# Experts with several row blocks, run one block at a time with small experts between, in a two-layer mixture-of-experts backbone

## The chip, the cores and the metric

The kernel runs on one core of one Trainium2 chip. The metric is the device time of one execution in microseconds (us); the kernel before is shown by the median of three runs. The profile is of one further execution. Engines are called by their names: TensorE (PE in the rows, PEld its weight loads), VectorE (DVE), ScalarE (ACT), GpSimd (POOL) and SyncE (SP), whose queue issues the weight loads.

## The reference

Two layers over 512 latent tokens and 256 context tokens of width 1024, all in float32. Each layer has a token mixer (projection, convolution, recurrence, output projection) and then a mixture of experts, which is what the change touches:

```python
gate = p_group * top_p / jnp.sum(top_p, axis=-1, keepdims=True)        # top-1 group of 4, top-2 of its 8 experts
...
def expert_block(args):
    x_blk, e = args
    a, u = jnp.split(x_blk @ w_gu[e], 2, axis=-1)                      # w_gu[e]: 1024 x 1024
    return (jax.nn.silu(a) * u) @ w_down[e]                            # w_down[e]: 512 x 1024
...
out = jnp.zeros((n_tok + 1, d), t.dtype).at[row_tok].add((yb * row_gate[:, None]).astype(t.dtype))
```

Layer 0 sends 768 tokens through two experts each, layer 1 only the 512 latent ones. Every one of the 32 experts' weights, 6 MB each, is read in each layer.

## The kernel before

The kernel runs mixer, routing and experts of layer 0, then the same of layer 1, then a last norm. In the routing, the experts are sorted on the chip by their number of rows, and each rank has a fixed room (`rooms`): in layer 0 rank 0 has 320 rows, rank 1 192, rank 2 128, ranks 3 to 5 96, ranks 6 to 15 64, ranks 16 to 28 32; in layer 1 rank 0 has 160, ranks 1 to 3 96, ranks 4 to 11 64, ranks 12 to 28 32. Three experts ("static") are not ranked; they are loaded while the routing still runs and computed first. Rows beyond a room go through `overflow`, a branch behind the last-but-one expert, whose count is tested at run time.

`units` cuts a rank's room into blocks of 128, then 64 and 32 rows: rank 0 of layer 0 is 128 + 128 + 64, rank 1 is 128 + 64, ranks 3 to 5 are 64 + 32. For a block, `rows_in` gathers its rows from the normed tokens in HBM (an indirect DMA of GpSimd, L1189) and transposes them on TensorE (L1211; VectorE copies the result to `xT`, L1213). `gate_up` multiplies them with four weight chunks (L1226 for 128 rows, L1230 for 64 or 32), `activate` makes silu(a) * u and transposes it (the h-transposes, L1244 for 128 rows, L1253 else; for 128 rows ScalarE and VectorE work first, L1239 to L1241), and `down` multiplies with the last two chunks (L1283 and L1295 in layer 0, L1321 and L1333 in layer 1). In layer 0 the result is scaled and scattered to HBM (L1181); in layer 1 the rows of several blocks of a kind are collected in one of three accumulators (`YB`) and added to the tokens by a matmul with a one-hot matrix (`merge`, L1369 to L1383).

An expert's weights are six chunks of 1 MB: four of gate and up, two of down. `load_chunks` issues them on SP in the program's order (L1162), each into a slot; `ring` takes slots from the head of a list and puts them back at its end, so a slot is used again when the others have been used, and its load waits on SP until the last matmul that reads it is done. The list has 16 slots in layer 0 (one more holds the modulation) and 17 in layer 1.

`moe` walks the ranks in `order`, a list by hand for each layer. For each expert, all its units are gathered and transposed, and each chunk is multiplied with all the units before the next chunk (`start`). In `end`, the units' activations come first, then their downs; before the last unit's down, `between` starts the next expert (its load on SP, its transposes and its first chunk), if `ahead` finds that the PSUM banks do (layer 0: fewer than three banks beside the first 128-block's own; layer 1: one unit of 64 or 32). The other three chunks of the next expert follow. SP alone is scheduled by hand (`manual_schedule`); the order of the other engines comes from the framework and follows the program closely. `flush` in layer 1 merges what is left of a kind when no unit of it is to come.

```python
    order = [[6, 16, 7, 17, 0, 18, 19, 1, 20, 21, 2, 22, 8, 3, 23, 9, 4, 24, 10, 5, 25, 11, 12, 26, 13, 14, 27, 15, 28],
             [4, 12, 5, 13, 0, 14, 15, 1, 16, 6, 17, 2, 18, 7, 19, 3, 20, 8, 21, 9, 22, 10, 23, 11, 24, 25, 26, 27, 28]]
```

Of the kernel before, what the change touches and what calls it, by code (L numbers as in the profile page):

```python
# [33 lines left out]
class Backbone:  # L34
# [1129 lines left out]
                self.tc.keep_in_program_order(o)  # L1164
        return list(tiles)

    def ring(self, n=6):

        out = []
        for _ in range(n):  # L1170
            pool, name = self.slots.pop(0)
            self.slots.append((pool, name))
            out.append(pool.tile([128, 2, D], F32, name=name))
        return out

# [124 lines left out]
    def down_here(self, kind, hT, dn, idx, pool, ps, last):  # L1300


        nc = self.nc
        tok, gate = idx
        f = 128 // kind
        w = D // f
        grp = self.groups.setdefault(kind, [])
        e = len(grp)
        if not grp:
            self.YB.append(self.YB.pop(0))  # L1310
            self.into[kind] = self.YB[-1]
        YB = self.into[kind]
        grp.append(tok)
        if len(grp) == f:
            self.tokens(kind, pool)
        if f == 1:
            for h in range(2):
                c = slice(512 * h, 512 * h + 512)
                py = ps.tile([128, 512], F32, name="acc", bufs=3)
                for k in range(4):  # L1320
                    nc.tensor.matmul(py, hT[k], dn[k // 2][:, k % 2, c], start=k == 0, stop=k == 3)  # L1321
                nc.vector.scalar_tensor_tensor(YB[:, c], py, gate, self.m5[:, c], op0=OP.mult, op1=OP.mult)
        else:
            py = ps.tile([128, 512], F32, name="acc", bufs=3)
            part = [(slice(kind * ((e - u) % f), kind * ((e - u) % f) + kind), slice(w * u, w * u + w)) for u in range(f)]
            for k in range(4):
                if k == 2 and last:

                    for _ in range(10):
                        nc.tensor.matmul(ps.tile([128, 512], F32, name="pS", bufs=2), self.onesb,  # L1330
                                         self.onesb[:, 0:1].to_broadcast([128, 512]), start=True, stop=True)
                for pr, c in part:
                    nc.tensor.matmul(py[pr, :w], hT[k], dn[k // 2][:, k % 2, c], start=k == 0, stop=k == 3)  # L1333
            for pr, c in part:
                nc.vector.scalar_tensor_tensor(YB[pr, c], py[pr, :w], gate[pr], self.m5[pr, c], op0=OP.mult, op1=OP.mult)
        if len(grp) == f:
            self.merge(kind, ps)
# [112 lines left out]
    def moe(self, l, stat, xp, mp, ps, ms2):  # L1450
        tc, nc, io = self.tc, self.nc, self.io
        if l:
# [5 lines left out]
            self.OT = mp.tile([128, 4, 512], F32R, name="OT")  # L1458
            self.YR = mp.tile([128, 2, D], F32R, name="YR")
            self.groups, self.into = {}, {}  # L1460
        left = [u[0] for r in self.order[l] for u in self.units(l, r)]

        def flush():

            for kind in list(self.groups):
                if kind not in left:
                    self.tokens(kind, mp)
                    self.merge(kind, ps)

        order = self.order[l]  # L1470
        ws = {}

        def load(n):
            if n not in ws:
                r = order[n]
                e = nc.sync.value_load(self.eid[0:1, r:r + 1], min_val=32 * l, max_val=32 * l + 31)
                ws[n] = self.load_expert(e, self.ring())

        def begin(n):
            load(n)  # L1480
            return self.start(ws[n], self.units(l, order[n]), xp, ps)

        N = len(order)
        for b in stat[:-1]:
# [2 lines left out]
        for n in range(-1, N):  # L1487

            nxt = []
            fits = n + 1 < N - 1 and self.ahead(l, self.units(l, order[n + 1]))  # L1490
            self.end(cur, mp, ps, n == N - 1, (lambda: nxt.append(begin(n + 1))) if fits else None)
            if l and n >= 0:
                for u in self.units(l, order[n]):
                    left.remove(u[0])
                flush()
            if n + 1 == N - 1:
                load(n + 1)
                self.overflow(l, xp, mp, ps, ms2)
            if n + 1 < N:
                cur, rest = nxt[0] if nxt else begin(n + 1)  # L1500
                rest()
# [105 lines left out]
    def dbgout(self, l, **k):  # L1607
        for n, t in k.items():
            if f"{n}{l}" in self.dbg:
# [7 lines left out]
             [160, 96, 96, 96] + [64] * 8 + [32] * 17 + [0] * 3]  # L1617

    static = [[7, 8, 9], [7, 8, 9]]
    order = [[6, 16, 7, 17, 0, 18, 19, 1, 20, 21, 2, 22, 8, 3, 23, 9, 4, 24, 10, 5, 25, 11, 12, 26, 13, 14, 27, 15, 28],  # L1620
             [4, 12, 5, 13, 0, 14, 15, 1, 16, 6, 17, 2, 18, 7, 19, 3, 20, 8, 21, 9, 22, 10, 23, 11, 24, 25, 26, 27, 28]]
    NOV = 28

    def plan(self):
# [141 lines left out]
```

## Time and profile before

| | |
|---|---|
| three runs | 2007.62, 2000.01, 2010.29 us; median 2007.62 |
| the profiled execution | 1996.57 us; span 1994.8 us |
| TensorE busy / its mean granted clock | 1700.2 us (85%) / 0.945 |
| VectorE, ScalarE, GpSimd busy | 914.0 (46%), 458.2 (23%), 394.3 us (20%) |
| moved by DMA | 542.35 MB, mean 272 GB/s |
| weight chunks into ring slots, issued by SP | 242 of gate/up, 121 of down, 1024 KB each |

The times of a row count from the start of the span. A row of the timeline gives start, duration, engine, line, operation, output and inputs, shape and number of instructions, and in brackets how long the engine was idle before it and what ended that. A float32 matmul of the program stands as two in the trace. Busy time of TensorE holds the pipelined ends of matmuls, which are modelled, so its share is no measure of its throughput. DMA share is the mean busy share of the core's 16 DMA engines.

### The profile page before, as it was taken

The numbers are of one execution on the slowest core, as the hardware profiler recorded it, in microseconds if no ns is written. First come the engines' busy times: TensorE is split into PE (matmuls) and PEld (weight loads), VectorE is DVE, ScalarE is ACT, GpSimd is POOL, SyncE is SP. The second block draws the span as 40 slices with busy tenths as digits, with TensorE's granted clock in tenths as the row PEclk, the third lists the DMA queues.
The fourth block names the chain that finished last, engine by engine and source line by source line (L and its number), as shares of the span: only waits on it lengthen the run. The fifth ranks groups of instructions, "written<-read, shape, count | busy, mean of one in ns | idle before, by whom it ended". The sixth has DMA issues, their size and how long they took to land. (4 is left out here: it accounts for less than half of the span.)

```text
span 1994.8 us, 33498 instructions
## 1 busy us (share of the span) xinstructions
PE 1700.2 (85%) x13488; PEld 1098.2 (55%) x13488; DVE 914.0 (46%) x2141; ACT 458.2 (23%) x897; POOL 394.3 (20%) x308
## 2 busy tenths in 40 slices
PE   5998999999968999888875899898968898888885
PEld 2766778798843444333332688777754344334342
DVE  4425255635664132222322637666563644445444
ACT  3512223323212122122211533333320100110011
POOL 1502212111122111111110632222111211111110
PEclk8999999999988999999987899999987999999998
DMA  7376562263489979999997322114478989999995
GB/s 276 101 271 212 179 212 76 76 242 90 168 326 374 418 317 379 417 416 418 417 419 298 135 82 57 54 43 157 137 280 324 417 342 417 418 417 418 417 418 241
DMA packets 141513, 542.35 MB, mean 272 GB/s; under 512 B 17394, under 2 KB 66720, under 8 KB 85417
## 3 DMA queue, kind: packets, MB, share of 16 engines
q1 hardware_dynamic: 118408, 466.17, 59.1%
q10 hardware_dynamic: 15040, 55.08, 8.0%
q0 software_dynamic: 7904, 18.90, 2.5%
q8 instruction: 108, 1.77, 0.4%
q14 instruction: 53, 0.43, 0.1%
HBM read 530.95 MB, written 15.96 MB: 274 GB/s over the span
## 5 line engine op out<-in xcount | busy, mean ns | idle before, releaser
L1230 PE MATMUL acc<-w,xT 128*32 128x256 f32 (+1 forms) x3360 | 378.4, 454 | 59.1 <-DVE xT L1213 34.6
L1230 PEld LDWEIGHTS acc<-w,xT 128*32 128x32 f32 (+1 forms) x3360 | 135.2, 119 | 260.6 <-issue 159.0
L322 POOL TENSOR_TENSOR hilo<-raw,hilo 128x1024 fp32r<-128x1024 f32 x64 | 157.3, 2463 | 436.4 <-ACT hilo L319 396.7
L333 PE MATMUL acc<-HA,hilo 128*128 128x384 f32 (+1 forms) x960 | 204.7, 355 | 0.0
L333 PE MATMUL acc<-HB,hilo 128*128 128x384 f32 (+1 forms) x960 | 202.4, 353 | 0.0
L333 PEld LDWEIGHTS acc<-HA,hilo 128*128 128x128 f32 x960 | 168.8, 189 | 16.2 <-issue 4.2
L333 PEld LDWEIGHTS acc<-HB,hilo 128*128 128x128 f32 x960 | 171.0, 190 | 9.2 <-issue 0.8
L1250 ACT COPY au<-acc 128x256 f32<-128x256 f32 (+1 forms) x69 | 31.1, 453 | 594.3 <-PE acc L1230 551.9
L345 PE MATMUL acc<-hilo,HA 128*128 128x512 f32 x504 | 131.2, 412 | 12.8 <-POOL HA L283 6.3
L1189 POOL DMA_INDIRECT xb<-h,idx x63 | 65.7, 1043 | 385.7 <-PE pS L1211 357.1
L345 PE MATMUL acc<-hilo,HB 128*128 128x512 f32 x504 | 125.8, 398 | 3.9 <-DVE hilo L322 3.6
L345 PEld LDWEIGHTS acc<-hilo,HA 128*128 128x128 f32 x504 | 97.9, 198 | 41.0 <-POOL HA L283 7.5
L1274 DVE SCALAR_TENSOR_TENSOR au<-w,gt,au 32x256 f32<-32x256 f32 (+2 forms) x102 | 58.6, 577 | 114.1 <-ACT au L1273 111.7
L319 ACT CAST hilo<-raw 128x1024 fp32r<-128x1024 f32 x80 | 83.5, 1049 | 119.1 <-PE acc L345 27.5
L345 PEld LDWEIGHTS acc<-hilo,HB 128*128 128x128 f32 x504 | 94.5, 190 | 29.1 <-DVE hilo L322 4.5
L1295 PE MATMUL acc<-w,hT 128*32 128x256 f32 (+1 forms) x816 | 97.2, 478 | 12.4 <-DVE hT L1258 6.4
L389 DVE TENSOR_TENSOR Q<-Q,Dk 128x256 f32<-128x256 f32 (+1 forms) x144 | 89.6, 651 | 23.7 <-PE pA L464 11.8
L1333 PE MATMUL acc<-w,hT 128*32 128x256 f32 (+1 forms) x896 | 87.4, 440 | 7.3 <-DVE hT L1258 5.2
L1181 POOL DMA_INDIRECT yb<-ys,idx x39 | 39.7, 1019 | 260.9 <-DVE ys L1297 185.3
L384 DVE TENSOR_TENSOR K<-K,Dk 128x768 f32<-128x768 f32 x64 | 72.9, 1139 | 21.5 <-ACT tmp L401 17.9
L1295 PEld LDWEIGHTS acc<-w,hT 128*32 128x32 f32 (+1 forms) x816 | 37.4, 126 | 69.5 <-issue 51.3
L1297 DVE TENSOR_TENSOR ys<-acc,au 128x256 f32<-128x256 f32 (+1 forms) x34 | 18.4, 542 | 124.9 <-PE acc L1295 124.5
(369 smaller groups left out, 2245.5 us busy)
## 6 DMA issues: line engine op xcount, KB each, us to landing
w<-in_w_e_gu SPq DMA_DIRECT2D x242, 1024.0 KB
w<-in_w_e_down SPq DMA_DIRECT2D x121, 1024.0 KB
adaw<-in_w_ada ACTq DMA_DIRECT2D x40, 1024.0 KB
raw<-in_w_in SPq DMA_DIRECT2D x64, 512.0 KB
adaw<-in_w_ada SPq DMA_DIRECT2D x8, 1024.0 KB
raw<-in_w_out SPq DMA_DIRECT2D x16, 512.0 KB
HA<-in_w_e_gu SPq DMA_DIRECT2D x6, 1024.0 KB
h<-SG SPq DMA_DIRECT2D x10, 512.0 KB
```

Of the source, the lines that this page charges most:

```text
L319: nc.scalar.copy(W[:, 0], w)
L322: eng.tensor_sub(W[:, 1], w, W[:, 0].bitcast(F32))
L333: nc.tensor.matmul(o, W[:, wi, k, :], H[k // 4][:, k % 4, hi, t], start=k == 0 and wi == hi, stop=k == 7 and wi == 1)
L345: nc.tensor.matmul(pa, H[k // 4][:, k % 4, hi, t], W[k // 2][:, wi, k % 2, :], start=k == ks[0] and wi == hi, stop=k == ks[-1] and hi == 1)
L384: nc.vector.tensor_tensor(half(Kv, TOK, 0, kn, b), half(Kv, TOK, 0, kn, b), vw(Dv, b, [[2 * b, n], [TOK - b, 2], [0, b]]), op=OP.mult)
L389: nc.vector.tensor_tensor(o, o, vw(Dv, (TOK + b) * d, [[2 * b, qn // (2 * b)], [0, b]]), op=OP.mult)
L1181: st = nc.gpsimd.indirect_dma_start(out=rows, out_offset=bass.IndirectOffsetOnAxis(ap=idx, axis=0), in_=yb, in_offset=None, bounds_check=r ...
L1189: self.nc.gpsimd.indirect_dma_start(out=xb, out_offset=None, in_=rows, in_offset=bass.IndirectOffsetOnAxis(ap=idx, axis=0), bounds_check=r ...
L1230: nc.tensor.matmul(pg[kind * u:kind * u + kind, :w], xT[k], gu[:, k % 2, w * u:w * u + w], start=st, stop=sp)
L1274: nc.vector.scalar_tensor_tensor(ms[pr, :o], self.m5s[pr, 0, c], g0[pr], ms[pr, :o], op0=OP.mult, op1=OP.add)
L1295: nc.tensor.matmul(py[kind * u:kind * u + kind, :w], hT[k], dn[k // 2][:, k % 2, w * u:w * u + w], start=k == 0, stop=k == 3)
L1333: nc.tensor.matmul(py[pr, :w], hT[k], dn[k // 2][:, k % 2, c], start=k == 0, stop=k == 3)
```

## The change

An expert that stands more than once in `order` is run one unit at a time: each time but the last it stands there takes its next unit, the last takes the rest. Its weights are loaded at its first step; their six slots are taken out of the ring's list (`keep`) and put back at its end after its last step. Experts between these steps use the slots that remain. In layer 0 the order is new: rank 1 stands twice (its 128 rows, then rank 23, then its 64), rank 0 three times (128; ranks 26, 17; 128; rank 16; 64), and all others have other places than before. In layer 1, rank 0 stands twice, with rank 14 between its 128 and its 32 rows; the rest is as before. The accumulator of a merge is now the first that no other kind is using.

```diff
-    def ring(self, n=6):
+    def ring(self, n=6, keep=None):
...
             pool, name = self.slots.pop(0)
-            self.slots.append((pool, name))
+            (self.slots if keep is None else keep).append((pool, name))
             out.append(pool.tile([128, 2, D], F32, name=name))
...
-            self.YB.append(self.YB.pop(0))
+            busy = [id(self.into[k]) for k in self.groups if k != kind]
+            self.YB.append(self.YB.pop([id(t) in busy for t in self.YB].index(False)))
...
-        left = [u[0] for r in self.order[l] for u in self.units(l, r)]
+
+        order, steps = self.order[l], []
+        for n, r in enumerate(order):
+            k, us = order[:n].count(r), self.units(l, r)
+            end = r not in order[n + 1:]
+            steps.append((r, us[k:] if end else us[k:k + 1], end))
+        left = [u[0] for st in steps for u in st[1]]
...
-        ws = {}
+        ws, kept = {}, {}
 
         def load(n):
-            if n not in ws:
-                r = order[n]
+            r = order[n]
+            if r not in ws:
                 e = nc.sync.value_load(self.eid[0:1, r:r + 1], min_val=32 * l, max_val=32 * l + 31)
-                ws[n] = self.load_expert(e, self.ring())
+                if not steps[n][2]:
+                    kept[r] = []
+                ws[r] = self.load_expert(e, self.ring(keep=kept.get(r)))
 
         def begin(n):
             load(n)
-            return self.start(ws[n], self.units(l, order[n]), xp, ps)
+            return self.start(ws[order[n]], steps[n][1], xp, ps)
...
-            fits = n + 1 < N - 1 and self.ahead(l, self.units(l, order[n + 1]))
+            fits = n + 1 < N - 1 and self.ahead(l, steps[n + 1][1])
             self.end(cur, mp, ps, n == N - 1, (lambda: nxt.append(begin(n + 1))) if fits else None)
-            if l and n >= 0:
-                for u in self.units(l, order[n]):
+            if n >= 0:
+                r, us, end = steps[n]
+                if end:
+                    self.slots += kept.pop(r, [])
+                for u in us:
                     left.remove(u[0])
-                flush()
+                if l:
+                    flush()
...
-    order = [[6, 16, 7, 17, 0, 18, 19, 1, 20, 21, 2, 22, 8, 3, 23, 9, 4, 24, 10, 5, 25, 11, 12, 26, 13, 14, 27, 15, 28],
-             [4, 12, 5, 13, 0, 14, 15, 1, 16, 6, 17, 2, 18, 7, 19, 3, 20, 8, 21, 9, 22, 10, 23, 11, 24, 25, 26, 27, 28]]
+
+
+    order = [[15, 24, 1, 23, 1, 6, 19, 3, 4, 18, 25, 12, 0, 26, 17, 0, 16, 0, 28, 2, 13, 7, 21, 10, 5, 14, 11, 9, 20, 8, 22, 27],
+             [4, 12, 5, 13, 0, 14, 0, 15, 1, 16, 6, 17, 2, 18, 7, 19, 3, 20, 8, 21, 9, 22, 10, 23, 11, 24, 25, 26, 27, 28]]
```

## Rows read from the trace of the kernel before

**Rows 1.** Windows: span, busy time (instructions) by engine; clock, DMA share, GB/s.

```profile
700.00:740.00 40.00, 35.84 (x248) 17.25 (x247) 16.56 (x30) 12.47 (x24) 8.10 (x8) 1.00 0.74 292
760.00:780.00 20.00, 18.50 (x78) 7.65 (x80) 6.88 (x12) 4.83 (x8) 3.04 (x3) 1.00 0.82 328
1620.00:1640.00 20.00, 18.00 (x134) 9.52 (x132) 11.35 (x38) 1.80 (x4) 3.56 (x3) 1.00 0.59 226
```

**Rows 2.** TensorE's waits, the longest group, in 616:1003 and then in 1003:1088.

```profile
PE acc L1230 <- DVE xT L1213: 17.4, 18, 1.5
...
PE acc L1230 <- DMA w<-in_w_e_gu: 14.3, 5, 5.5
```

**Rows 3.** TensorE's timeline in layer 0, h-transposes of single steps.

```profile
626.05 0.75 PE L1253 MATMUL pS<-ident,au 128*128 128x128 f32 x4 [0.69 <-ACT au L1250]
636.62 0.51 PE L1253 MATMUL pS<-ident,au 128*128 128x128 f32 x2 [0.55 <-ACT au L1250]
...
661.16 0.51 PE L1253 MATMUL pS<-ident,au 128*128 128x128 f32 x2 [0.55 <-ACT au L1250]
...
730.10 0.50 PE L1253 MATMUL pS<-ident,au 128*128 128x128 f32 x2 [0.49 <-ACT au L1250]
...
737.73 0.51 PE L1253 MATMUL pS<-ident,au 128*128 128x128 f32 x2 [0.54 <-ACT au L1250]
...
783.06 0.50 PE L1253 MATMUL pS<-ident,au 128*128 128x128 f32 x2 [0.49 <-ACT au L1250]
...
790.69 0.51 PE L1253 MATMUL pS<-ident,au 128*128 128x128 f32 x2 [0.54 <-ACT au L1250]
...
814.27 1.13 PE L1244 MATMUL pS<-ident,au 128*128 128x128 f32 x4 [2.88 <-DVE au L1241]
...
829.81 0.51 PE L1253 MATMUL pS<-ident,au 128*128 128x128 f32 x2 [0.49 <-ACT au L1250]
...
842.01 0.74 PE L1253 MATMUL pS<-ident,au 128*128 128x128 f32 x4 [0.74 <-ACT au L1250]
...
861.19 1.07 PE L1253 MATMUL pS<-ident,au 128*128 128x128 f32 x6
...
874.09 0.51 PE L1253 MATMUL pS<-ident,au 128*128 128x128 f32 x2 [0.49 <-ACT au L1250]
...
975.22 0.75 PE L1253 MATMUL pS<-ident,au 128*128 128x128 f32 x4 [0.74 <-ACT au L1250]
...
990.31 0.75 PE L1253 MATMUL pS<-ident,au 128*128 128x128 f32 x4 [0.74 <-ACT au L1250]
```

**Rows 4.** TensorE's timeline at the end of layer 0's experts.

```profile
1053.23 3.42 PE L1230 MATMUL acc<-w,xT 128*64 128x512 f32 x8 [5.55 <-DMA w<-in_w_e_gu]
...
1082.48 0.50 PE L1253 MATMUL pS<-ident,au 128*128 128x128 f32 x2 [0.53 <-ACT au L1250]
1085.21 1.93 PE L1295 MATMUL acc<-w,hT 128*32 128x256 f32 x32 [2.23 <-DVE hT L1258]
```

**Rows 5.** SP's timeline: issues of four chunks, from the first's start to the last's end.

```profile
696.39 30.87 SPq L1162 DMA_DIRECT2D w<-in_w_e_gu  x4
...
984.49 8.40 SPq L1162 DMA_DIRECT2D w<-in_w_e_gu  x4
...
1000.40 9.14 SPq L1162 DMA_DIRECT2D w<-in_w_e_gu  x4
...
1607.71 27.96 SPq L1162 DMA_DIRECT2D w<-in_w_e_gu  x4
```

**Rows 6.** DMA issues: count, size of each, median us from issue to landing.

```profile
w<-in_w_e_down POOLq DMA_DIRECT2D x2, 1024.0 KB, 6.1
```

**Rows 7.** TensorE's timeline in layer 1, rank 0 and the first wait for weights.

```profile
1598.42 3.60 PE L1226 MATMUL pA<-w,xT 128*128 128x512 f32 x8
...
1634.20 1.93 PE L1333 MATMUL acc<-w,hT 128*32 128x256 f32 x32
...
1943.15 1.43 PE L1230 MATMUL acc<-w,xT 128*32 128x256 f32 x16 [2.96 <-DMA w<-in_w_e_gu]
```

More of the change, by code (lines that the diff above doesn't have):

```diff
@@ L1468, in flush @@
                     self.merge(kind, ps)
-        order = self.order[l]
-        ws = {}
+        ws, kept = {}, {}
         def load(n):
-            if n not in ws:
-                r = order[n]
+            r = order[n]
+            if r not in ws:
                 e = nc.sync.value_load(self.eid[0:1, r:r + 1], min_val=32 * l, max_val=32 * l + 31)
-                ws[n] = self.load_expert(e, self.ring())
+                if not steps[n][2]:
+                    kept[r] = []
+                ws[r] = self.load_expert(e, self.ring(keep=kept.get(r)))
         def begin(n):
             load(n)
-            return self.start(ws[n], self.units(l, order[n]), xp, ps)
+            return self.start(ws[order[n]], steps[n][1], xp, ps)
         N = len(order)
```

## The prediction

> **What bounds the kernel now.** The shares of the whole span say little, so I read by stretch. Each mixture-of-experts stretch (layer 0 from about 616 to 1087 us, layer 1 from 1536 to 1974) is fed by one stream of 1 MB weight chunks, six to an expert. First look at the windows [rows 1]: between the ends of these stretches the DMA share is 1.0 but for three places, 0.74 over 40 us, 0.82 and 0.59 over 20 us each. These holes are worth 10.4 + 3.6 = 14.0 us in layer 0 and 8.2 us in layer 1, and each follows an expert with many rows (ranks 0 and 1 of layer 0, rank 0 of layer 1). Then ask who is late. In the sums of TensorE's waits [rows 2] the first 387 us of layer 0 have seven groups and none is a weight's landing; the largest is the copy of the transposed rows. Only after 1003 us does TensorE wait for weights, 14.3 us in five waits. So until 1003 TensorE is behind the stream, the ring is full, and a hole is the stream waiting for a slot; behind 1003 small experts let TensorE catch up and the stream ends the layer. Both limits lie close together: a change that closes holes but makes TensorE slower gains nothing.
>
> **Price of a step on TensorE.** The step of one unit is best priced from one unit's h-transposes to the next step's [rows 3], because everything, waits too, lies in between: 32 rows after 32 take 7.6 us (730.10 to 737.73), 64 after 32 12.2, 32 after 64 10.6, 64 after 64 15.1, 96 after 64 19.2, 32 after 96 12.9. Rank 2, the only 128-block that runs alone, takes 23.6 from the 32 before it and 15.5 to the 32 after it. Rank 1 (128 and 64 together) takes 45.3 from 32 to 32 and rank 0 (128, 128, 64 together) 68.9. Subtract 7.6 for the pair of 32s: a lone 128-block costs 31.5 us, a 64 between 32s 15.2; but rank 0 in company costs 61.3, which leaves (61.3 - 15.2) / 2 = 23.0 for each of its blocks. The 8.5 us between them is the wait that another unit's matmuls cover when they stand beside it (2.88 us for VectorE in front of rank 2's transposes [rows 3]), and a hand-over to the next step.
>
> **The change in layer 0: TensorE.** The order before has 28 transitions (32 to 64 seven, 64 to 32 five, 64 to 96 and 96 to 32 three each, 32 to 32 and 64 to 64 two each, ranks 0, 1 and 2 as above), and their prices sum to 433 us: 626.0 + 433 = 1059.4 for the last expert's h-transposes, which ran at 1082.5 [rows 4]. The 23.1 us between are the weight waits, slow matmuls behind them and the overflow branch; they are TensorE's slack. The order after has 31 transitions: 64 to 32 six times, 32 to 128, 128 to 32, 32 to 32 three times each, 32 to 64 five, 64 to 64 four, 64 to 96 and 96 to 32 once; five are not in the trace and are put together from the pieces of their neighbours (32 to 96 18.0, 96 to 96 21.5, 64 to 128 24.7, 128 to 64 19.3, 96 to 64 15.7, each good to some 2 us). The sum is 456 us, 23 more: three blocks more run alone, with three hand-overs more. So without a single wait for weights TensorE would be at 626 + 456 = 1082 us, where it is now with all its waits. Slack that was there is used up.
>
> **The stream in layer 0.** A chunk takes 15.9 / 6 = 2.65 us (two experts' issues start at 984.49 and 1000.40 [rows 5]; gathers and scatters are in that). The ring has 16 slots here. Six that are kept leave ten, or 26.5 us of stream, and unlike in rank 2's case now no chunk is given back as the block goes along. I worked the new order forward chunk by chunk: TensorE's instants from the prices above, the slots in the order of the code, a chunk starting when the one before is through and 2 us after its slot was last read. The 2 us is an estimate: [rows 6] gives 6.1 us from issue to landing of one chunk, less 2.65 of transfer, so 0 to 3.5. Example: 0b's h-transposes come at 857.5; expert 16's first chunk is read 4 us later and its second behind 0b's down, at 871; expert 28's chunks 4 and 5 need just these slots while the stream is ready at 860 and 866, which makes holes of 3.3 and 6.7 us. All pieces: 13.1 us in five holes around rank 1, 21.8 in six around rank 0, together 35. The same working gives 16.8 and 6.3, together 23, for the order before (SP's issues for rank 1's first four chunks indeed stretch over 30.87 us [rows 5]; the DMA shares show less, as gathers fill part of a hole). So the holes grow by 12 us. The stream before ends at 1053.2 (expert 15's first chunk, by TensorE's wait [rows 4]) plus 11 chunks, 1082.4; after, at 1094. The last down, 2 us, then ends at 1096 against 1087.1 before [rows 4]: **+9 us**. Bounds: the 128-block as in company and all slack used, -14; stream and TensorE both late by the full 23, +20.
>
> **A rule against the rows.** The rows put TensorE behind the stream until 1003 us. The Trainium skill (Perfetto Trace Analysis, section Optimization Strategy) says that where the most contended engine changes over time, interleaving the regimes may help; by that the holes close and the change is worth up to 22 us, by the rows it loses.
>
> **Layer 1.** Only rank 0 (128 + 32) is split, around expert 14. Before, its matmuls start at 1598.4, each 128-part of a chunk taking 3.6 us; chunks 0 to 3 come free as they are read, and the fourth issue of expert 1 waits until 1607.7 + 28 = 1635.3 because chunks 4 and 5 are read last by the 32-block's down at 1634.2, behind the merge [rows 5, 7]. After: 1598 + 4 x 3.5 for the block alone, 2.9 + 1.1 for its wait and transposes, then expert 14's first chunk is read at 1618; down and merge follow, and 14's other chunks are read between 1629 and 1639. The ring has 11 of 17 slots; expert 15's chunk 5 wants 14's first (hole 3 us), expert 1's first wants 14's second (8), later ones 3: 14 us against 9 to 10 by the same working before. TensorE itself is 3.3 us later behind the split (7.6 for one more 32-step, less 4.3 gained in front, as the 32-part no longer stands beside the block). It waited for weights at 1943 [rows 7], so the stream sets the end: **+4.5 us**, bounds 0 and +8 (a hole as long as 128-block and merge; none at all would be -8).
>
> **What costs nothing.** Weights are loaded once per expert as before, so DMA issues, register loads on SP and bytes stay; SP's later issues only move with their slots. Gathers and scatters stay at one per unit, on POOL, which is idle most of both stretches; if it were late, the copy of transposed rows would be. The choice of the accumulator for merges and the list of what is left change the program's building, not instructions. No wait is added on purpose; the one that appears is SP's, in order, and every later weight stands behind it.
>
> **Sum.** 9 + 4.5 = 13.5 us. The profiled execution took 1996.6 us, span 1994.8, 11 us under the median of 2007.6; the difference is added to the median: 2021 us.
>
> **Rivals.** (1) *Slack takes it.* The five composed prices and the holes are 2 us too long each, TensorE's 23 us go where it waited anyway, and the stream's holes only move. For: the limits lie within a few us. Against: the holes lie before 910 us, the slack after 1003. Layer 0 +2, layer 1 +2: 2012 us. Decides: whether weight waits after 1003 are still about 14 us. (2) *The split pays.* The scheduler puts the next expert's transposes and first chunk into a lone block's wait, so that it costs 23 instead of 31.5; three blocks give back 25 us, TensorE ends near 1057 without waits, and stays close enough to the stream that ten slots suffice. Then the holes close: up to 14 + 8 us, with two thirds of it -14: 1994 us. Decides: the wait in front of the 128-block's h-transposes, under 1 us. Against: rank 2 has the same program order today and waits 2.88 us. The page's rule would come true in this way. (3) *Nothing moves*, because the merged program keeps the block's units together: 2008 us; nothing in the diff speaks for it.
>
> **How the numbers follow.** A difference of 0.5%, some 10 us, is what a measurement of this kernel can tell from no change. Forecast 0.50, a fifth of it still under +10; rival 1 0.30, of which 0.04 ends above +10; rival 2 0.16, of which 0.02 gains less than 10; rival 3 0.04. So slower 0.40 + 0.04 = 0.44, same 0.10 + 0.26 + 0.02 + 0.04 = 0.42, faster 0.14. The forecast's own range is +7 to +24 (2014 to 2032), from the bounds of the 2 us and of the composed prices; rival 1 and a part of rival 2 take the low end to 2000.
>
> **What would show it.** Right: h-transposes of 128-blocks with a wait near 2.9 us four times in layer 0; SP issues that wait for downs of small experts beside ranks 0 and 1; DMA windows under 0.9 around 685 to 715 and 860 to 910; weight waits of TensorE in layer 0 under 10 us; in layer 1 a hole around 1620 to 1635 longer than before. Wrong: DMA share of 1.0 through both split experts, or a last h-transpose of layer 0 before 1080.

## The result and the profile after

The change makes the kernel slower by half a per cent: median 2015.47 us against 2007.14 us of before (20 runs each), ratio 1.0052 with a 95% interval of 1.0041 to 1.0064, which is 8.2 to 12.8 us with 10.4 in the middle. The medians themselves lie 8.3 us apart. The forecast was +13.5 us.

| | before | after |
|---|---|---|
| profiled execution's span, us | 1994.8 | 2012.0 |
| layer 0, from the first ranked expert's h-transposes to the last's | 456.4 | 460.2 |
| layer 1, from the second's to the last's | 409.4 | 412.9 |
| TensorE's waits for weights in layer 0 | 14.3 | 11.0 |
| DMA time lost in layer 0's holes, layer 1's hole | 14.0, 8.2 | 18.6, 11.7 |

The two spans must not be subtracted: they differ by 17.2 us, but 9.65 of these are there before the changed part begins (626.05 against 635.70 us at the first ranked expert), gathered in code that the change leaves alone. So I compare stretches, each from one instruction to another of the same kernel. These are the windows of both stretches, first of the kernel before, then of the changed one (span, busy time by engine, clock, DMA share, GB/s).

```profile
626.05:1082.48 456.43, 390.44 (x2611) 166.35 (x2611) 122.64 (x242) 85.47 (x167) 69.44 (x67) 0.94 0.97 397
1559.19:1968.61 409.42, 345.32 (x2893) 164.70 (x2893) 190.87 (x524) 38.62 (x86) 57.42 (x51) 0.98 0.99 407
```

```profile
635.70:1095.89 460.19, 385.80 (x2611) 164.86 (x2611) 122.88 (x242) 85.42 (x167) 69.04 (x67) 0.95 0.97 394
1572.99:1985.91 412.92, 348.44 (x2892) 165.17 (x2892) 190.91 (x524) 38.67 (x86) 57.24 (x51) 0.97 0.98 403
```

The instructions are the same. In layer 0 TensorE is no busier (385.80 against 390.44 us, at a clock 0.01 higher); what grew is the time in which it stands, 66.0 to 74.4 us. The next view says at what it stands: TensorE's waits in the changed kernel, in 616:1003 and then in 1003:1110 (us in total, times, longest).

```profile
PE acc L1230 <- DVE xT L1213: 15.0, 18, 1.5
PE pS L1244 <- DVE au L1241: 11.5, 4, 2.9
PE acc L1230 <- DMA w<-in_w_e_gu: 4.8, 1, 4.8
...
PE acc L1230 <- DMA w<-in_w_e_gu: 6.2, 2, 3.1
```

The second line is the one to see. It is the wait of a 128-block's h-transposes for VectorE; before it was 3.3 us in two waits, and it has become 11.5 us in four. The longest group of before [rows 2], the copies of the rows, is nearly as it was. The waits for weights are shorter in sum (11.0 against 14.3) and one of them now stands before 1003 us. On TensorE's timeline the four waits, the prices around them and the end of layer 0 look so (they answer to [rows 3] and [rows 4]):

```profile
635.70 0.75 PE L1253 MATMUL pS<-ident,au 128*128 128x128 f32 x4 [0.69 <-ACT au L1250]
...
669.83 1.06 PE L1244 MATMUL pS<-ident,au 128*128 128x128 f32 x4 [2.88 <-DVE au L1241]
683.97 0.51 PE L1253 MATMUL pS<-ident,au 128*128 128x128 f32 x2 [0.49 <-ACT au L1250]
...
818.61 0.74 PE L1244 MATMUL pS<-ident,au 128*128 128x128 f32 x4 [2.88 <-DVE au L1241]
...
840.57 0.51 PE L1253 MATMUL pS<-ident,au 128*128 128x128 f32 x2 [0.55 <-ACT au L1250]
862.49 0.74 PE L1244 MATMUL pS<-ident,au 128*128 128x128 f32 x4 [2.88 <-DVE au L1241]
876.99 0.51 PE L1253 MATMUL pS<-ident,au 128*128 128x128 f32 x2 [0.49 <-ACT au L1250]
...
923.22 1.13 PE L1244 MATMUL pS<-ident,au 128*128 128x128 f32 x4 [2.88 <-DVE au L1241]
...
1070.44 1.94 PE L1230 MATMUL acc<-w,xT 128*32 128x256 f32 x16 [3.10 <-DMA w<-in_w_e_gu]
...
1095.89 0.50 PE L1253 MATMUL pS<-ident,au 128*128 128x128 f32 x2 [0.54 <-ACT au L1250]
```

The blocks at 669.83 (rank 1), 818.61 and 862.49 (rank 0) are the three that the split made lonely, the one at 923.22 is rank 2, which was alone before too. Each waits 2.88 us.

Then the stream. Windows of the changed kernel, answering to [rows 1], and under them the two longest of SP's issues of down chunks inside these windows (start, time from the first issue's start to the last's end):

```profile
690.00:720.00 30.00, 25.61 (x170) 9.95 (x166) 7.33 (x13) 5.11 (x9) 5.24 (x5) 1.00 0.82 309
860.00:920.00 60.00, 51.13 (x316) 23.01 (x316) 15.51 (x30) 9.87 (x20) 8.21 (x8) 0.94 0.78 306
1620.00:1650.00 30.00, 25.57 (x132) 12.12 (x134) 10.22 (x21) 3.07 (x6) 4.55 (x4) 0.94 0.61 243
```

```profile
865.42 9.75 SPq L1162 DMA_DIRECT2D w<-in_w_e_down  x2
...
1612.01 19.90 SPq L1162 DMA_DIRECT2D w<-in_w_e_down  x2
```

The holes around rank 1 (30 x 0.18 = 5.4 us) and rank 0 (60 x 0.22 = 13.2) make 18.6 us, where before had 10.4 and 3.6. In layer 1 it is 30 x 0.39 = 11.7 against 8.2. An issue of two chunks that takes much longer than their transfer (2 x 2.65 us) is SP standing in front of a slot that isn't free, with every later weight behind it; [rows 5] shows the same for the order before. The first ends at 875.2 us: two chunks of expert 28 have waited for the slots of expert 16's first two chunks, and the second of these is read only behind the down of rank 0's second block (from 873.70). It is the very example that the prediction worked out.

### The profile page after: what moved, and what is told of

The parts are those of the page before. It is cut to its first block, busy times and chain, and to the rows that moved or that the text cites. A ratio compares the mean times of both kernels' runs of the same rounds, so it can differ in the third digit from the quotient of the medians.

```text
span 2012.0 us, 33480 instructions
## 1 busy us (share of the span) xinstructions
PE 1702.9 (85%) x13488; PEld 1099.6 (55%) x13488; DVE 915.1 (45%) x2141; ACT 458.2 (23%) x897; POOL 392.9 (20%) x308
## 5 line engine op out<-in xcount | busy, mean ns | idle before, releaser
L389 DVE TENSOR_TENSOR Q<-Q,Dk 128x256 f32<-128x256 f32 (+1 forms) x144 | 89.8, 653 | 24.5 <-PE pA L464 11.7
L1213 DVE COPY xT<-pS 128x256 f32<-128x256 f32 (+1 forms) x79 | 42.5, 539 | 63.8 <-PE pS L1211 63.5
```

Of the source, the lines that this page charges most:

```text
L389: nc.vector.tensor_tensor(o, o, vw(Dv, (TOK + b) * d, [[2 * b, qn // (2 * b)], [0, b]]), op=OP.mult)
L1213: nc.vector.tensor_copy(t[:, :n].rearrange("p a b -> p (a b)"), pt[:, :128 * n])
```

## The experiments

A stretch below is always the one of the table above. A ratio is always to runs of the kernel before on the same chip.

**1. Are the two layers' losses independent?** Two kernels are the changed one with one layer's order put back, layer 0's in the first and layer 1's in the second:

```diff
-    order = [[15, 24, 1, 23, 1, 6, 19, 3, 4, 18, 25, 12, 0, 26, 17, 0, 16, 0, 28, 2, 13, 7, 21, 10, 5, 14, 11, 9, 20, 8, 22, 27],
+    order = [[6, 16, 7, 17, 0, 18, 19, 1, 20, 21, 2, 22, 8, 3, 23, 9, 4, 24, 10, 5, 25, 11, 12, 26, 13, 14, 27, 15, 28],
```

```diff
-             [4, 12, 5, 13, 0, 14, 0, 15, 1, 16, 6, 17, 2, 18, 7, 19, 3, 20, 8, 21, 9, 22, 10, 23, 11, 24, 25, 26, 27, 28]]
+             [4, 12, 5, 13, 0, 14, 15, 1, 16, 6, 17, 2, 18, 7, 19, 3, 20, 8, 21, 9, 22, 10, 23, 11, 24, 25, 26, 27, 28]]
```

> Layer 0 keeps the order of before, layer 1 has the split of rank 0. My theory (each layer pays for its own split: a lone block on TensorE and six slots less for the stream): layer 0's stretch, from the first ranked expert's h-transposes to the last one's, stays at 456.4 us as before, layer 1's is 426.3 as after (422.2 before); +4 us in all, ratio 1.002. Rival A (the new sequence of layer 0 makes the loss, the splits are free): layer 1 at 422, ratio 1.000. Rival B (the split of layer 1 by itself closes its hole of 8 us and the loss in it after comes from what layer 0 hands over): layer 1 at 416, ratio 0.997.

> Layer 0 has the new order with its three steps more, layer 1 the order of before. My theory: layer 0's stretch 460 us as after (456.4 before), layer 1's 422; +4 us, ratio 1.002. If the layers' losses add, this ratio and that of the split of layer 1 alone multiply to the 1.0052 of the whole change. Rival (the two losses are not independent): layer 1 over 424, ratio over 1.004.

Layer 1's split alone: 1.0016 (1.0004 to 1.0029), layer 1 412.8 us. Layer 0's new order alone: 1.0026 (1.0009 to 1.0042), layer 0 463.0 us. Both lose, and 0.16 + 0.26% come near the 0.52% of the whole. The runs also show how far one stretch scatters: the old order of layer 0 took 456.4 and 453.6 us in two kernels, the new one 460.2 and 463.0, so **layer 0 lost 6.6 us** by the means, give or take some 3. Layer 1 is steadier: 409.3 to 411.0 in five kernels with the old order (mean 409.7), 412.8 and 412.9 with the new one, so **+3.1 us** (3.5 in the pair of the table). Together 9.7, near the 10.4 of the ratio. (The two expectations count layer 1 from one step earlier, the first ranked expert: 422.2 before, 426.3 after. So counted, it is 426.2 in the first kernel and 423.8 in the second.)

**2. Sequence or split?** Layer 0's change does two things: it sorts the experts otherwise, and it splits ranks 0 and 1. One kernel takes the new sequence with ranks 0 and 1 standing once, the other the old sequence with splits; layer 1 is as before in both.

```diff
-    order = [[15, 24, 1, 23, 1, 6, 19, 3, 4, 18, 25, 12, 0, 26, 17, 0, 16, 0, 28, 2, 13, 7, 21, 10, 5, 14, 11, 9, 20, 8, 22, 27],
+    order = [[15, 24, 1, 23, 6, 19, 3, 4, 18, 25, 12, 0, 26, 17, 16, 28, 2, 13, 7, 21, 10, 5, 14, 11, 9, 20, 8, 22, 27],
```

```diff
-    order = [[15, 24, 1, 23, 1, 6, 19, 3, 4, 18, 25, 12, 0, 26, 17, 0, 16, 0, 28, 2, 13, 7, 21, 10, 5, 14, 11, 9, 20, 8, 22, 27],
+    order = [[6, 16, 7, 17, 0, 18, 0, 19, 0, 20, 1, 21, 1, 22, 2, 8, 3, 23, 9, 4, 24, 10, 5, 25, 11, 12, 26, 13, 14, 27, 15, 28],
```

> Layer 0 has the new sequence of experts, but ranks 0 and 1 stand once, at their first places, with all their units together; no slots are kept. Layer 1 as before. My theory (the split costs, the sequence is neutral): TensorE's sum of steps is as before but for neighbours, the holes behind ranks 0 and 1 are as before, 14 us by the DMA share; stretch 452 to 458 us, ratio 0.998 to 1.001. Rival A (the sequence costs): 460 us or more, ratio 1.002 or more.

> Layer 0 has the sequence of before with the splits put in: rank 0 as 128, 18, 128, 19, 64 and rank 1 as 128, 21, 64 with rank 20 ahead of it; layer 1 as before. My theory (the split costs): three lone blocks more at 31.5 instead of 23 us and the ring of ten slots, 23 us of TensorE against 23 of slack: stretch 460 to 468 us, ratio 1.002 to 1.006. Rival A (only the new sequence costs): 456 us, ratio 1.000. Rival C (the split pays where small experts stand on both sides, and it is the new sequence that spoils it): under 450, ratio under 0.997.

The sequence alone is no loss, rather a small gain that the interval doesn't settle: 0.9989 (0.9973 to 1.0004), layer 0 451.4 us. The split in the old sequence costs twice the whole change, more than any of its theories said: 1.011 (1.0092 to 1.0127), layer 0 473.9 us. So the split is the part that loses, about 10 us in the new sequence (461.6, the mean of two, against 451.4) and 19 in the old one (473.9 against 455.0), and the new sequence makes it bearable.

**3. TensorE or the stream?** In three kernels every weight load behind the first ones brings only 64 of the 1024 columns into the same tile. So a share of the weights is left out, and what is left of layer 0 is TensorE's own time. (The rest of the edit keeps each slot's tile, so that its other columns stay. Each kernel has one run.) Their layer 1 isn't compared, as other values there choose other experts.

```diff
...
+            elif getattr(self, "thin", False):
+                w = w[:, :, 0:64]
+                o = self.nc.sync.dma_start(w, src[i, r:r + 256, 0:64].rearrange("a (p k) f -> p (a k) f", p=128))
+                continue
             o = (q or self.nc.sync).dma_start(w, src[i, r:r + 256, :].rearrange("a (p k) f -> p (a k) f", p=128))
```

> The kernel before, but in the expert stretches only the first load of each slot is whole, every later one brings 64 of 1024 columns into the same tile; the weights that are multiplied are thus not the expert's own. TensorE's work is the same and the stream never late. My theory: layer 0's stretch is what the prices of the steps sum to, 433 us plus or minus 4 (456.4 before), so some 20 us of it are waits for the stream and their slow matmuls. Rival B (the stream sets nothing, all is TensorE): 452 or more.

> The changed kernel with the same thin loads. My theory: the change puts TensorE's own work in layer 0 up by 15 to 23 us, stretch 448 to 456 us, and in layer 1 by 3 us against the thin kernel before. Rival B (TensorE's price is small, the six kept slots and the holes make the loss): up by less than 8 us in layer 0, 441 or less, and by less than 1 in layer 1.

> The split in the old order of layer 0 (ranks 0 and 1 with one small expert between their blocks), with the later loads bringing 64 of 1024 columns, so the stream never waits: the output is not the reference's, since the weights are partly left out. This measures TensorE's own time in layer 0 with that order; 442.5 before and 452.1 after in the same way. Theory (splits that stand next to each other cost the stream most): 450 to 456, so 18 to 24 of the 473.9 measured with full loads are waits for weights. Rival (the old order is dear on TensorE itself): 465 or more.

Layer 0's window before, after and in the old sequence with splits:

```profile
634.20:1076.66 442.46, 386.82 (x2611) 164.37 (x2611) 122.57 (x242) 85.53 (x167) 69.24 (x67) 0.95 0.21 61
```

```profile
635.10:1087.15 452.05, 386.24 (x2610) 166.28 (x2610) 122.88 (x242) 85.50 (x167) 69.01 (x67) 0.95 0.21 59
```

```profile
632.98:1092.94 459.96, 392.12 (x2610) 167.08 (x2611) 122.47 (x242) 85.49 (x167) 69.05 (x67) 0.94 0.20 57
```

TensorE's wait for VectorE in front of the 128-blocks' h-transposes (616:1003) with thin loads, before and after (the edit adds ten lines, so L1244 is L1254 here):

```profile
PE pS L1254 <- DVE au L1251: 3.3, 2, 2.9
```

```profile
PE pS L1254 <- DVE au L1251: 11.5, 4, 2.9
```

With the DMA share at 0.2 the stream is out of the game, and TensorE needs 442.5 us before and 452.1 after: **+9.6 us**, of which the lone blocks' waits are 11.5 - 3.3 = 8.2. Both expectations were missed: 442.5 lies between the 433 and the 452 of the two theories, 9.6 between 15 and 8. The accounts close to some 3 us, which is the scatter of a stretch: 442.5 + 14.3 of waits for weights is 456.8 (456.4 measured), 452.1 + 11.0 is 463.1 (460.2 measured), and 452.1 + 8.5 is 460.6 for the kernel with layer 0's new order alone (463.0 measured). So after the change TensorE works 9.6 us longer and waits 3 to 6 us less for weights. The third kernel went against what I expected of it (450 to 456): with splits in the old sequence TensorE alone needs 460.0, which is 17.5 more, and that is nearly all of the 17.5 to 19 that the full loads showed. So the old sequence with splits is dear on TensorE. That it is cheap on the stream isn't shown: with full loads its holes grow too, to 27.6 us by the DMA share between 720 and 840 us. Why it costs TensorE 8 us more than the new sequence was not tried apart.

**4. What does the short ring cost by itself?** The sequence without splits, but the six slots of ranks 0 and 1 go back to the ring only after the small experts between which the changed kernel would have put the blocks. So the ring is short and no block is lonely.

```diff
-                if not steps[n][2]:
+                if l == 0 and r in (0, 1):
                     kept[r] = []
...
-                if end:
+                if l == 0:
+                    self.slots += kept.pop({23: 1, 16: 0}.get(r), [])
+                elif end:
                     self.slots += kept.pop(r, [])
```

> The sequence without splits, but the six slots of rank 1 go back only after the small expert behind it, and those of rank 0 only after the three small ones behind it: the ring is short where the split makes it short, with no lone block on TensorE. Theory (the split's cost is TensorE's lone blocks and the late pieces of the stream, some half each): layer 0 454 to 457 against 451.4 without the kept slots and 460.2 with the split; DMA windows 690 to 720 and 860 to 920 at 0.8 again. Rival (all of it is the lone blocks): 451 to 452, no holes there. Rival (all of it is the short ring): 459 to 461.

Missed by every theory: ratio 1.0066 (1.0043 to 1.0089), layer 0 471.2 us, 20 more than without the kept slots and 10 more than with the split. These are the windows of rank 0's stretch without kept slots, and then with them, and then TensorE's waits for weights with them (616:1003):

```profile
820.00:855.00 35.00, 33.29 (x156) 14.83 (x154) 12.00 (x19) 8.48 (x15) 6.00 (x6) 1.00 0.56 215
```

```profile
824.00:860.00 36.00, 34.69 (x160) 14.77 (x158) 11.64 (x18) 7.40 (x13) 6.01 (x6) 1.00 0.30 103
```

```profile
PE acc L1230 <- DMA w<-in_w_e_gu: 21.1, 8, 5.7
```

The hole grows from 35 x 0.44 = 15.4 to 36 x 0.70 = 25.2 us, a second one of 6.0 us (671 to 686, DMA share 0.60) opens around rank 1, where there was none, and TensorE's waits for weights in layer 0 from 12.7 to 33.1 (21.1 and another 12.0 behind 1003). Without its waits for weights TensorE needs 471.2 - 33.1 = 438.1 here and 451.4 - 12.7 = 438.7 there: by this account all of the loss is the stream. What I hadn't seen is that keeping the slots and putting small experts between the blocks belong together. With the whole rank at one go and its chunks kept, nothing is given back for the length of three units; with the split the small experts in between give their slots back and the stream goes on, losing 13.2 us there instead of 25.2. So the interleaving does help the stream, but no more than it pays for the slots that it keeps: without split and kept slots the same hole is 15.4 us.

**5. Can the lone block's wait be covered?** In the changed kernel, a lone 128-block hands the next step's first work over ahead of its activation:

```diff
+        if between is not None and [u[0] for u in units] == [128]:
+            between()
+            between = None
         act = lambda j: self.activate(units[j][0], pg[j], pool, ps)
```

> The changed kernel, but ahead of the activation of a lone 128-block the next expert's transposes and first chunk are run, so that they stand in the wait before its h-transposes. My theory (the lone block's uncovered wait is a large part of the loss): the wait of 2.88 us falls to under 1 in front of all four lone blocks of layer 0 and of the one in layer 1 that has a next expert to start; stretch of layer 0 452 to 456 us, of layer 1 407 (from the second to the last h-transposes 412.9 before this edit, 409.4 in the kernel before the change), ratio 1.000 to 1.002. Rival B (kept slots): layer 0 at 459 or more, ratio 1.004 or more.

Ratio 1.0041 (1.0024 to 1.0059), layer 0 459.7 us: no difference to the changed kernel that can be told, and what rival B said. But the edit did what it says for only two of the four lone blocks of layer 0, and not for the one in layer 1. These are rank 1's block, where it did not, and rank 0's second block, where it did, and then the sum of such waits in 616:1003, which was 11.5 us in four:

```profile
669.46 1.10 PE L1244 MATMUL pS<-ident,au 128*128 128x128 f32 x4 [2.98 <-DVE au L1241]
670.49 1.94 PE L1230 MATMUL acc<-w,xT 128*32 128x256 f32 x16
...
863.73 0.72 PE L1244 MATMUL pS<-ident,au 128*128 128x128 f32 x4 [0.30 <-DVE au L1241]
```

```profile
PE pS L1244 <- DVE au L1241: 6.3, 3, 3.0
```

At rank 1 the rows' transposes stand no longer between (670.49 follows at once), but the next expert's chunk is still behind the h-transposes, and they wait 2.98 us; rank 0's first block waits 2.97. Why TensorE didn't get the program's order there was not tried. Rank 0's second block waits 0.30 us, and rank 2's not at all. What a covered wait is worth can be read around rank 0's second block, from the h-transposes of expert 17 to those of expert 16, first with this edit and then in the changed kernel, at the same granted clock:

```profile
840.04:874.40 34.36, 31.55 (x160) 14.83 (x160) 8.71 (x16) 5.22 (x11) 3.94 (x4) 0.95 0.97 400
```

```profile
840.57:876.99 36.42, 31.02 (x160) 14.26 (x160) 8.71 (x16) 5.22 (x11) 4.04 (x4) 0.95 0.85 346
```

It comes to 2.1 us, most of the 2.6 by which the wait is shorter. Around rank 2 (from expert 28's h-transposes to expert 13's) it is 6.0 us, 36.95 for 42.90, and there the granted clock differs too. These are the 6.34 us from rank 2's h-transposes on, in the changed kernel, behind a wait of 2.88 us, and with the edit, behind none:

```profile
923.22:929.56 6.34, 5.55 (x16) 2.35 (x17) 1.35 (x2) 1.21 (x2) 1.24 (x1) 0.51 1.03 428
```

```profile
923.08:929.42 6.34, 6.34 (x20) 2.95 (x20) 1.44 (x2) 1.21 (x2) 0.00 (x0) 1.00 1.01 416
```

The clock of the first is near 1.2 GHz, the lower of its two levels; behind the three other waits of the changed kernel it is 0.55 (669.83 to 673.61), 0.75 (818.61 to 821.91) and 0.88 (862.49 to 865.31). So a lone block's wait can cost more than itself. Yet layer 0 isn't shorter. At expert 20's h-transposes TensorE is 2.9 us ahead of the changed kernel (412.2 against 415.1 us behind the first ranked expert's), but its last wait for weights ends where it did (434.3 against 434.7), and its waits for weights behind 1003 us are 9.6 us instead of 6.2: the stream sets the end, and it came no earlier. What four covered waits would be worth stays open.

**6. Does the split pay when TensorE is less late?** One edit takes the largest of TensorE's waits away, in any of the kernels: the next expert's rows are transposed ahead of the current expert's activation, so that their copies are done when its first chunk begins.

```diff
-            self.end(cur, mp, ps, n == N - 1, (lambda: nxt.append(begin(n + 1))) if fits else None)
+            xT = self.rows_of(steps[n + 1][1], xp, ps) if fits else None
+            self.end(cur, mp, ps, n == N - 1, (lambda: nxt.append(begin(n + 1, xT))) if fits else None)
```

> The kernel before, without any split, but the transposes of the next expert's rows stand ahead of the activation's h-transposes wherever the next expert may start early, so that they fill the wait for ScalarE and their copy is done in time. My theory (TensorE behind the stream makes the holes, not the shape of the experts): each step is some 0.9 us shorter, 20 us and more per layer of TensorE; the holes of layer 0 fall from 14 us by the DMA share to under 8 and the stream then ends the layer: stretch 440 to 446 us, layer 1 402 to 406, ratio 0.988 to 0.993. Rival (holes come from ranks 0 and 1 holding their slots, whatever TensorE does else): stretch 453 or more, ratio 0.998 or more.

> The changed kernel with the one edit of before_rows_early: the next expert's row transposes stand ahead of the activation of the current one. Theory (TensorE is late, and what the split costs is TensorE's time plus two late pieces of the stream): the waits for the rows' copies go, so TensorE gains some 10 us in layer 0 as before_rows_early did (456.4 to 447.1), but the lone blocks keep their 2.9 us waits and the stream its holes around ranks 1 and 0: layer 0 450 to 456, layer 1 409 to 411, ratio to the kernel before 0.998 to 1.002, so 0.002 to 0.006 above before_rows_early. Rival (interleaving pays once TensorE has time to spare): layer 0 at or under 447, ratio at or under 0.996.

> The new sequence of layer 0 with ranks 0 and 1 once, layer 1 as before, and the row transposes ahead. Theory (two gains that both come from TensorE being less late): the sequence alone gave 451.4 against 456.4 in layer 0, the early rows 447.1; together 444 to 447, where the stream is the limit (442.5 with the loads thinned), and layer 1 408; ratio 0.993 to 0.997. Rival (they remove the same lateness): 447 and 0.996, as with the early rows alone.

| kernel with early rows | ratio to before | layer 0, us | layer 1, us |
|---|---|---|---|
| before | 0.9962 (0.9944 to 0.998) | 447.1 | 408.0 |
| after | 0.9994 (0.9974 to 1.0014) | 456.4 | 410.4 |
| new sequence, no split | 0.9946 (0.9924 to 0.9968) | 450.0 | 409.7 |

TensorE's waits in layer 0 with early rows, first in the kernel before (616:1003 and then 1003:1110), then in the changed one (616:1003):

```profile
PE acc L1230 <- DMA w<-in_w_e_gu: 9.4, 7, 4.1
...
PE acc L1230 <- DVE xT L1213: 0.5, 1, 0.5
...
PE acc L1230 <- DMA w<-in_w_e_gu: 15.7, 5, 5.9
```

```profile
PE pS L1244 <- DVE au L1241: 10.3, 4, 3.0
...
PE acc L1230 <- DMA w<-in_w_e_gu: 2.0, 1, 2.0
```

The 17.4 us of [rows 2] fall to 0.5, waits for weights now stand ahead of 1003 us too, and layer 0 gets 8 us shorter than the old order's mean of 455.0, somewhat less than expected (447.1 and 0.9962, where 440 to 446 and 0.988 to 0.993 were said): now TensorE stands ready oftener and the stream is the limit. This was the case in which interleaving should have paid. It doesn't: with the split, layer 0 takes 456.4 instead of 447.1, the four waits for VectorE stand (10.3 us), and the ratio is 0.3% above the same edit without split, as the theory had it. Early rows and the new sequence together give 0.9946, the fastest of all, but its interval overlaps with that of early rows in the kernel before, and its layer 0 (450.0) missed the 444 to 447 expected. Both beat the kernel before and the changed one; which is the better is not settled.

## Why the prediction was right

**The direction and the mechanism.** The four steps of "what would show it" that name a place came true there, one of them in part: 2.88 us four times; SP standing in front of slots around ranks 1 and 0, though more for the gate and up matmuls of the small experts (32.7 us in 665:725, 35.7 in 860:920) than for their downs, which the sign named (12.0 and 14.2); DMA windows of 0.82 and 0.78 where under 0.9 was said; the longer hole in layer 1. One sign was missed narrowly: weight waits under 10 us were said, 11.0 came in the changed kernel (8.5 in the one with only layer 0's new order).

**TensorE, +23 us forecast, +9.6 measured.** This term was mis-sized. It doesn't stand in the sum itself, but TensorE's instants set the working of the stream. The order after was summed too high, mostly by one price: 64 after 64 was taken as 15.1 us from a single pair, but it is 13.4 in the changed kernel. The windows of the pair in the kernel before, then of one in the changed kernel, show why:

```profile
975.22:990.31 15.09, 13.44 (x57) 4.78 (x57) 3.54 (x6) 2.41 (x5) 2.02 (x2) 0.89 1.01 418
```

```profile
696.17:709.56 13.39, 11.74 (x57) 4.39 (x57) 3.54 (x6) 2.41 (x5) 2.12 (x2) 1.00 0.63 225
```

The same 57 matmuls took 13.44 and 11.74 us, at a granted clock of 0.89 and 1.00: the pair was priced in a stretch where the clock was partly down, and four such transitions stand in the new order, of 13.3 to 13.4 us each. 32 after 128 was 14.1 and 14.5 us (from 669.83 to 683.97, from 862.49 to 876.99) instead of 15.5. And the 23.1 us that the prediction called TensorE's slack held only 14.3 us of waits for weights. Most of the rest is the last expert's step, which stands behind the overflow branch in both kernels but was priced like any other, at 10.6 and 7.6 us. It begins with these rows, of the kernel before and of the changed one, and ends at 1082.48 [rows 4] and 1095.89:

```profile
1064.56 0.75 PE L1253 MATMUL pS<-ident,au 128*128 128x128 f32 x4 [0.74 <-ACT au L1250]
```

```profile
1081.16 0.50 PE L1253 MATMUL pS<-ident,au 128*128 128x128 f32 x2 [0.55 <-ACT au L1250]
```

That is 17.9 and 14.7 us without any wait for weights, 7.3 and 7.1 more than priced: no slack, and nothing in the difference. Less these 7 us, TensorE's own time with thin loads is some 435 us before, where 433 was priced, and 445 after, where it was 456. So the price of the order before was good and that of the new one 11 us too high. What is left of the 8.5 us per lone block is above all the visible 2.88.

**Layer 0, +9 us forecast, +6.6 measured.** The forecast had holes that grow by 12 us, so a stream that ends 12 us later, and 3 us less behind it. The windows of the result show growth of only 4.6 us (14.0 to 18.6). But the two kernels of experiment 1 are a second pair with the old and the new order of layer 0. These are their windows around ranks 0 and 1, first with the old order and then with the new:

```profile
706.00:746.00 40.00, 35.63 (x254) 17.95 (x254) 17.78 (x33) 11.55 (x23) 9.12 (x9) 1.00 0.81 322
766.00:786.00 20.00, 18.02 (x115) 7.80 (x114) 7.45 (x12) 5.20 (x10) 4.02 (x4) 1.00 0.84 333
```

```profile
690.00:720.00 30.00, 26.01 (x174) 10.18 (x170) 7.34 (x13) 4.82 (x8) 4.48 (x5) 0.99 0.76 288
860.00:920.00 60.00, 50.74 (x313) 22.76 (x312) 15.50 (x30) 10.17 (x20) 8.20 (x8) 0.91 0.74 289
```

Here the holes grow by 12.0 us, from 7.6 + 3.2 = 10.8 to 7.2 + 15.6 = 22.8; by the means of the two pairs, 8.3. The end of the stream can be told as the prediction told it, by TensorE's wait at the first chunk of the last expert but one. In the second pair these waits are, old order and new:

```profile
1056.33 3.38 PE L1230 MATMUL acc<-w,xT 128*64 128x512 f32 x8 [5.54 <-DMA w<-in_w_e_gu]
```

```profile
1073.92 1.93 PE L1230 MATMUL acc<-w,xT 128*32 128x256 f32 x16 [3.26 <-DMA w<-in_w_e_gu]
```

Counted from the first ranked expert's h-transposes, that is 424.4 and 438.0 us, 13.6 later; in the first pair 427.2 [rows 4] and 434.7, 7.6 later. The mean is 10.6, and behind this mark the layer is 4 us shorter in both pairs, which gives the 6.6. So the step was right, and its size within what two pairs can tell. In part that is luck: the two workings whose difference it is gave 23 us for the order before and 35 for the new one, where the windows show 14.0 and 10.8, and 18.6 and 22.8; both are too long by about as much. The end came out between the forecast and rival 1, which said that slack takes it: 3.3 to 5.8 of TensorE's 9.6 us did go into waits that were there before (14.3 to 11.0, or to 8.5).

**Layer 1, +4.5 us forecast, +3.1 measured.** In the pair of the result the hole grew by 3.5 us and the stretch by the same. TensorE's timeline shows the block alone, and its wait as worked out, with 2.20 us instead of 2.9; SP's long issue at 1612.01 ends at 1631.9, when expert 14's first chunk has been read, as forecast for expert 15's last chunk:

```profile
1611.88 14.00 PE L1226 MATMUL pA<-w,xT 128*128 128x512 f32 x32
...
1628.08 0.74 PE L1244 MATMUL pS<-ident,au 128*128 128x128 f32 x4 [2.20 <-DVE au L1241]
```

(The working's 1607.7 + 28 is 1635.7, not 1635.3; nothing hangs on it.)

**The rivals.** Rival 2, the split pays, falls: its deciding wait was 2.88 us and not under 1, and the split loses in the old sequence, in the new one and with early rows. The rule of the Trainium skill (Perfetto Trace Analysis, section Optimization Strategy), that interleaving regimes may help where the most contended engine changes over time, brought no gain in time here (1.0052); experiment 4 shows the part of it that is true, a stream that loses 13.2 us instead of 25.2 once slots are kept. Rival 3 is out, since the split stands in the trace. Rival 1 was true in part, as said, but not by the sign that it named: the waits for weights behind 1003 us are not still about 14 us but 6.2. By its medians the result is 8.3 us over before, nearly halfway between rival 1's 4.5 and the forecast's 13.5; by the ratio, 10.4, it is nearer the forecast.

## What to carry to other kernels

When two limits lie within a few us of each other, closing one's holes with work that makes the other later gains nothing: find which is late, and shorten that first (here, moving the transposes of the next rows ahead gave 0.9962 with no change of order). A block that runs alone shows the hand-over between engines that its neighbours used to cover, so count the blocks that become lonely and price each by such a wait in the trace. A growth of some us read from one pair of profiles can be off by more than half (the holes grew by 4.6 us in one pair and 12.0 in another), so a term of that size wants more than one pair. A price should be read together with the granted clock of its own stretch, and a step that has something else in it, as the last one with its branch, wants a price of its own.

## What was not expected of the hardware

TensorE's clock enters every price. In the kernel of experiment 5 the down of rank 1's lone block (672.35) takes 8.71 us, in the changed kernel (673.61) the same 16 matmuls take 7.09; the granted clock was 0.82, a mix of the two levels, 1.2 and 2.4 GHz, and 1.00. The windows of the two (each counts 8 matmuls more, of the chunks beside it), with TensorE having waited 2.98 and 2.88 us shortly before:

```profile
672.35:681.06 8.71, 8.71 (x24) 3.67 (x24) 0.93 (x2) 0.00 (x0) 1.01 (x1) 0.82 1.01 420
```

```profile
673.61:680.70 7.09, 7.09 (x24) 2.98 (x20) 0.69 (x1) 0.00 (x0) 1.00 (x1) 1.00 1.02 419
```

So busy time scatters by itself. The new order of layer 0 keeps TensorE busy for 385.80 us at a clock of 0.95 in the changed kernel, and in the kernel with layer 0's new order alone for 391.51 at 0.94:

```profile
635.95:1098.97 463.02, 391.51 (x2611) 166.80 (x2611) 122.86 (x242) 85.43 (x167) 69.05 (x67) 0.94 0.96 391
```

That is as much as the 4.6 us by which TensorE was less busy after than before in the table's pair, which therefore says nothing of the change.

Whether that clock belongs to the kernel or to the chip it ran on was not tried. The time that TensorE stands is steadier: 66.0 and 66.3 us in the two kernels with the old order, 74.4 and 71.5 in the two with the new one.
